# Roots of norms by Newton steps on token partitions in the attention stage of a Hymba layer

## The chip, the cores and the metric

The kernel runs on one core of one Trainium2 chip. The metric is the device time of one execution in microseconds (us). The engines are TensorE (PE; its weight loads are listed as PEld), VectorE (DVE), ScalarE (ACT), GpSimd (POOL) and SyncE (SP, which here starts DMA transfers). Each engine works through its own queue in order and waits on semaphores for the others.

## The reference

One layer with two feed-forward blocks around two groups of attention heads, all in float32, on 1024 tokens and 16 meta tokens. What matters here are the norms behind the two groups:

```python
def rmsnorm(x, g):
    xf = x.astype(jnp.float32)
    y = xf * lax.rsqrt(jnp.mean(xf * xf, axis=-1, keepdims=True) + EPS)
    return (y * g.astype(jnp.float32)).astype(x.dtype)
...
    p = jax.nn.softmax(s, axis=-1)
    a = p[:, :, 0] - lam * p[:, :, 1]            # differential attention, 4 heads
...
    o = rmsnorm(o, sub_gain) * (1.0 - lambda_init)   # per head, over its 128 features
...
    out_b = rmsnorm(out_b, win_norm[l])              # window group, over 512 features
    h = h + jnp.concatenate([out_a, out_b], axis=-1) @ w_out[l]
```

## The kernel before

All large products are made of three products of rounded parts: each factor is split into a high part (a cast) and a low part (a subtraction), and hi·hi, lo·hi and hi·lo are added in PSUM. Activations lie transposed: features on the 128 partitions, tokens along the free axis. The program is written with a framework whose scheduler orders each engine's queue; tiles of one name share a ring of buffers.

The change lies in the differential stage, which the profiled execution passes at 1060 to 1331 us. Its loop takes one step `i` for each of 32 query tiles (4 heads × 8 tiles) and four more. A step issues:

- the scores of a tile, `ds` (L780, PE), the row minimum `dmx` (L784, DVE), the exponential `dp` with its sum (L786, ACT), and one step later the difference of the two softmaxes (L791 and L794 on DVE, L793 on POOL);
- the transposes `dt` of the difference of an earlier tile (L1167, L1175, PE) and their copies to `at` (L1170 on DVE, L1172 and L1176 on ACT);
- in every second step the products with the values, `do<-at,v` (L1183), copied to the head's `oh` (L1186, ACT); in the other steps, from step 9, a piece of `out_win`, the products of the window group with its output weights (`do<-ow_hi,owhi` and so on, L167), whose results DVE adds to `hrm` (L114);
- at i = 4 and 8 the norm of one half of the window group (`own`, four tiles of 128 features), and from i = 7, every fourth step, the norm of half a head (`oh`, 512 tokens).

`do` and `dt` have one PSUM buffer each; `do` is shared by the values, the window-out products and the sums of the norms.

A norm before: ACT squares the tile (`nacc`; for the window group POOL adds four of them), PE multiplies the result with a matrix of ones (L1092, 128x512), so that every partition has the sum of its token. ACT takes the root (`nr`, L1097, Abs_reciprocal_sqrt), for which its table is loaded, and the exponential's table is loaded again afterwards. ACT squares the root (`nt`, L1101), and two DVE operations correct it by a Newton step (L1102, L1103). POOL multiplies the tile by the root (L1112, L1122), ACT makes the high part with the gain (L1114, L1124), DVE the low part (L1115, L1125). For heads 0 to 2 ACT copies the sums of both halves to `nv` (L1139), and one root of 1024 columns serves the pair; head 3 has a root for each half. Behind the loop the remaining `fill` steps follow, and then the output products of the differential group (`po`, L167); `s`, `wal` and `wah` are the parts of the next block's weights, which SP loads (`s<-wu`).

Of the kernel before, what the change touches and what calls it, by code (L numbers as in the profile page):

```python
# [10 lines left out]
F32 = mybir.dt.float32  # L11
F32R = mybir.dt.float32r
AF = mybir.ActivationFunctionType
ALU = mybir.AluOpType
# [4 lines left out]
P = 128  # L19
# [32 lines left out]
def layer(  # L52
# [40 lines left out]
    gains = const("gains", [P, 4, KT])  # L93
    eps = cpool.tile([P, 1], F32, name="eps")
    nc.vector.memset(eps, EPS)
    warm = cpool.tile([P, 1], F32, name="warm")
    nc.scalar.activation(warm, eps, AF.Abs_reciprocal_sqrt)
    nc.vector.tensor_scalar(gains, gains, -0.5 / D, None, op0=ALU.mult)

    wgain = const("wgain", [P, 4])  # L100
    dgain = const("dgain", [P, 1])
    nc.vector.tensor_scalar(wgain, wgain, -0.5 / 512, None, op0=ALU.mult)
    nc.vector.tensor_scalar(dgain, dgain, -0.5 / P * (1.0 - LAMBDA_INIT), None, op0=ALU.mult)

    neglam = cpool.tile([P, 1], F32, name="neglam")

# [6 lines left out]
    def tt(eng, out, a, b, op):  # L113
        eng.tensor_tensor(out, a, b, op=op)  # L114

    def split(hi, lo, src, eng=None):
        nc.scalar.copy(hi, src)  # L117
        tt(eng or nc.vector, lo, src, hi.bitcast(F32), ALU.subtract)
# [953 lines left out]
    owp = Rings(st_o, "ow").reserve("owraw").reserve("owhi", 2).reserve("owlo", 2)  # L1072
    with ExitStack() as st:
        op = Rings(st, "op").reserve("ow_hi").reserve("ow_lo")
        npool = Rings(st, "dn")
        psum = Rings(st, "dps", space=PSUM).reserve("do").reserve("dt")
        ds1 = Rings(st, "ds1", space=PSUM).reserve("ds")

        ow_hi = op.tile([P, 4, SEQ], F32R, name="ow_hi")
        ow_lo = op.tile([P, 4, SEQ], F32R, name="ow_lo")  # L1080

        def sums(srcs, n):
            acc = npool.tile([P, 512], F32, tag="nacc", name="nacc")[:, :n]
            for i, s in enumerate(srcs):
                if i == 0:
                    nc.scalar.activation(acc, s, AF.Square)
                else:
                    sq = npool.tile([P, 512], F32, tag="nsq", name="nsq")[:, :n]
                    nc.scalar.activation(sq, s, AF.Square)
                    nc.gpsimd.tensor_tensor(acc, acc, sq, op=ALU.add)  # L1090
            ps = psum.tile([P, 512], F32, tag="do", name="do")[:, :n]
            nc.tensor.matmul(ps, ones, acc, start=True, stop=True)  # L1092
            return ps

        def rsqrt(v, n, width):
            r = npool.tile([P, SEQ], F32, tag="nr", name="nr")[:, :n]
            nc.scalar.activation(r, v, AF.Abs_reciprocal_sqrt, bias=eps, scale=1.0 / width)  # L1097
            for c0 in range(0, n, 512):
                vc, rc = v[:, c0 : c0 + 512], r[:, c0 : c0 + 512]
                t = npool.tile([P, 512], F32, tag="nt", name="nt")  # L1100
                nc.scalar.activation(t, rc, AF.Square)  # L1101
                nc.vector.scalar_tensor_tensor(t, vc, EPS * width, t, op0=ALU.add, op1=ALU.mult)  # L1102
                nc.vector.scalar_tensor_tensor(rc, t, -3.0 * width, rc, op0=ALU.add, op1=ALU.mult)  # L1103
            return r

        def win_norm(c):
            c0, n = CH_REAL[c]
            ow = npool.tile([P, 4, 512], F32, tag="own", name="own")
            nc.sync.dma_start(ow, ow_d[:, :, c0 : c0 + n])
            r = rsqrt(sums([ow[:, t, :] for t in range(4)], n), n, 512)  # L1110
            for t in range(4):
                nc.gpsimd.tensor_tensor(ow[:, t, :], ow[:, t, :], r, op=ALU.mult)  # L1112
                hi = ow_hi[:, t, c0 : c0 + n]
                nc.scalar.mul(hi, ow[:, t, :], wgain[:, t : t + 1])  # L1114
                nc.vector.scalar_tensor_tensor(  # L1115
                    ow_lo[:, t, c0 : c0 + n], ow[:, t, :], wgain[:, t : t + 1], hi.bitcast(F32),
                    op0=ALU.mult, op1=ALU.subtract,
                )

        def head_scale(hd, c, o, r):  # L1120
            c0, n = CH_REAL[c]
            nc.gpsimd.tensor_tensor(o, o, r, op=ALU.mult)  # L1122
            hi = o_hi[:, hd, c0 : c0 + n]
            nc.scalar.mul(hi, o, dgain)  # L1124
            nc.vector.scalar_tensor_tensor(  # L1125
                o_lo[:, hd, c0 : c0 + n], o, dgain, hi.bitcast(F32), op0=ALU.mult, op1=ALU.subtract
            )

        nvs = {}

        def head_norm(hd, c, oh):
            os = [oh[:, c0 : c0 + n] for c0, n in CH_REAL]
            ps = sums([os[c]], 512)
            if hd == 3:
                head_scale(hd, c, os[c], rsqrt(ps, 512, P))
                return
            if c == 0:
                nvs[hd] = npool.tile([P, SEQ], F32, tag="nv", name="nv")
            nc.scalar.copy(nvs[hd][:, c * 512 : (c + 1) * 512], ps)  # L1139
            if c == 1:  # L1140
                r = rsqrt(nvs[hd], SEQ, P)
                for j in range(2):
                    head_scale(hd, j, os[j], r[:, j * 512 : (j + 1) * 512])

        def out_win(m, c, ws):
            if c == 0:
# [51 lines left out]
        for i in range(NQ + 4):  # L1198
            work, tg = None, iter(())
            steps = []  # L1200

            def do_scores(c):
                if N_EARLY <= i < NQ:
                    scores(heads[i // NB], i % NB, c, sc[i], ds1 if c else ds0)

            def do_combine():
                if N_EARLY < i <= NQ:
                    pend[i - 1] = combine(*sc.pop(i - 1))

# [24 lines left out]
            do_scores(0)  # L1234
            do_scores(1)
            do_combine()
            for z in range(3):
                do_t()
                if z < 2:
                    do_w()  # L1240
            if i < NQ and i % NB == 4 and i // NB + 1 < 4:
                heads[i // NB + 1] = load_head(i // NB + 1)
            if i in (4, 8):
                win_norm(i // 8)
            if i >= 7 and (i - 7) % 4 == 0:
                hd2, c = divmod((i - 7) // 4, 2)
                head_norm(hd2, c, ohs[hd2])
        for _ in fill:
            pass

# [165 lines left out]
```

## Time and profile before

| | |
|---|---|
| time, median of 3 runs | 2071.48 us (2070.87 to 2072.05) |
| profiled execution | 2074.79 us, its span 2072.9 us |
| mean granted TensorE clock | 0.981 of full speed |
| PE busy in the span | 1943.9 us (94%) |
| DVE, ACT, POOL busy | 1279.3 (62%), 879.4 (42%), 960.3 (46%) us |
| of it in 1066 to 1331 us: PE | 232.25 of 265 us |
| DVE, ACT, POOL there | 178.60, 163.44, 104.24 us |

Busy times are those of instructions on the engine; a matmul's end is modelled. The span runs from the first to the last instruction, the time of an execution also has what lies around it. The last two lines are the stage of the change.

### The profile page before, as it was taken

How to read it: one execution, taken by the hardware profiler on the slowest of the kernel's cores; microseconds unless marked ns; L12 is line 12 of the kernel's file. 1: busy time of each engine (PE TensorE's matmuls, PEld its weight loads, DVE VectorE, ACT ScalarE, POOL GpSimd, SP SyncE). 2: the span in 40 equal slices, each digit the busy share in tenths (PEclk: the TensorE clock that was granted, in tenths of full speed). 3: DMA queues.
4: the chain of work that ended last, by engine and by line, in shares of the span. 5: the costliest groups of instructions: out<-in, count | busy, mean ns of one | idle time of the engine just before them, and what ended most of it. 6: DMA issues, size and time to landing. Idle time of an engine off the chain costs nothing.

```text
span 2072.9 us, 30356 instructions
## 1 busy us (share of the span) xinstructions
PE 1943.9 (94%) x11484; PEld 1692.1 (82%) x11484; DVE 1279.3 (62%) x1853; ACT 879.4 (42%) x1611; POOL 960.3 (46%) x807
## 2 busy tenths in 40 slices
PE   5999999998999989899978999898999999989998
PEld 4999999998999879777756777676778888877877
DVE  7855554548875660376766777477665555487745
ACT  6433333334432431366566666354333333344433
POOL 0565454545443740576456432003655554454443
PEclk9999999999999999999988999999999999999999
DMA  5332322328422351544442321622323223375122
GB/s 172 108 109 98 120 92 97 109 92 319 155 64 81 133 174 52 143 122 123 105 113 67 97 85 39 203 102 81 124 106 122 95 89 117 130 282 167 61 82 82
DMA packets 106003, 244.14 MB, mean 118 GB/s; under 512 B 14209, under 2 KB 29009, under 8 KB 105857
## 3 DMA queue, kind: packets, MB, share of 16 engines
q1 hardware_dynamic: 94336, 204.53, 31.1%
q0 software_dynamic: 11520, 37.67, 4.6%
q8 instruction: 90, 1.47, 0.3%
q14 instruction: 57, 0.46, 0.1%
HBM read 169.86 MB, written 65.44 MB: 114 GB/s over the span
## 4 chain that ended last, share of the span: by engine, by line
PE 70%; DVE 11%; DMA 6%; ACT 5%; POOL 3%; issue 3%; SPq 1%; DVEq 0%; POOLq 0%; ACTq 0%
PE p L226 35%; PE pA L577 7%; PE pj L167 5%; PE pC L577 3%; PE pv L884 3%; PE pd L167 2%; PE ds L780 2%; DVE bl L114 2%; PE po L167 2%; PE do L1183 2%; PE pB L577 2%; PE do L167 1%; DMA ru<-wu 1%; POOL s L114 1%; ACT dp L786 1%
## 5 line engine op out<-in xcount | busy, mean ns | idle before, releaser
L114 POOL TENSOR_TENSOR s<-ru 128x512 f32<-128x512 f32 x42 | 55.9, 1331 | 264.5 <-DMA ru<-wu 190.1
L226 PE MATMUL p<-b_hi,wal 128*128 128x260 f32 (+1 forms) x528 | 141.5, 323 | 5.7 <-DVE wal L114 5.7
L226 PE MATMUL p<-b_hi,wah 128*128 128x260 f32 (+1 forms) x528 | 143.2, 325 | 3.6 <-ACT wah L117 1.6
L226 PE MATMUL p<-t_hi,wch 128*128 128x260 f32 (+1 forms) x528 | 141.2, 321 | 5.7 <-DVE u L114 5.7
L226 PE MATMUL p<-b_lo,wah 128*128 128x260 f32 (+1 forms) x528 | 142.5, 322 | 3.4 <-DVE b_lo L114 3.4
L226 PE MATMUL p<-t_lo,wch 128*128 128x260 f32 (+1 forms) x528 | 141.0, 321 | 0.0
L226 PE MATMUL p<-t_hi,wcl 128*128 128x260 f32 (+1 forms) x528 | 140.8, 321 | 0.0
L226 PE MATMUL p<-t_lo,wbh 128*128 128x260 f32 (+1 forms) x504 | 135.5, 319 | 0.0
L226 PE MATMUL p<-t_hi,wbl 128*128 128x260 f32 (+1 forms) x504 | 133.4, 320 | 0.0
L226 PE MATMUL p<-t_hi,wbh 128*128 128x260 f32 (+1 forms) x504 | 133.1, 320 | 0.0
L114 DVE TENSOR_TENSOR u<-p,m 128x520 f32<-128x520 f32 (+1 forms) x88 | 61.0, 693 | 116.5 <-PE p L226 108.9
L117 ACT CAST wbh<-s 128x512 fp32r<-128x512 f32 x84 | 52.1, 621 | 164.9 <-PE p L226 142.1
L577 PE MATMUL pA<-bh,wh 128*128 128x260 f32 (+1 forms) x432 | 115.3, 322 | 2.6 <-DVE h L584 2.6
L577 PE MATMUL pA<-bl,wh 128*128 128x260 f32 (+1 forms) x432 | 114.7, 319 | 0.0
L117 ACT CAST wah<-rg 128x512 fp32r<-128x512 f32 x88 | 53.9, 620 | 143.0 <-PE p L226 112.1
L577 PE MATMUL pA<-bh,wl 128*128 128x260 f32 (+1 forms) x432 | 111.9, 319 | 1.8 <-POOL wl L114 1.8
L114 DVE TENSOR_TENSOR wal<-rg,wah 128x512 fp32r<-128x512 f32 x88 | 74.0, 847 | 63.6 <-ACT wah L117 63.6
L114 DVE TENSOR_TENSOR bl<-r,bh 128x520 fp32r<-128x520 f32 (+1 forms) x126 | 109.0, 900 | 3.3 <-ACT bh L117 2.6
L117 ACT CAST wch<-ru 128x512 fp32r<-128x512 f32 x88 | 54.7, 621 | 130.5 <-PE p L226 72.6
L584 DVE SCALAR_TENSOR_TENSOR h<-pA,h 128x520 f32<-128x520 f32 (+1 forms) x96 | 66.1, 690 | 63.2 <-PE pA L577 63.1
L117 ACT CAST wh<-s 128x384 fp32r<-128x384 f32 x96 | 49.1, 513 | 130.1 <-PE pA L577 65.5
L114 POOL TENSOR_TENSOR s<-wr 128x384 f32<-128x384 f32 x48 | 55.4, 1157 | 100.6 <-DVE wl L114 89.7
(290 smaller groups left out, 6113.2 us busy)
## 6 DMA issues: line engine op xcount, KB each, us to landing
rg<-wg SPq DMA_DIRECT2D x44, 512.0 KB, 3.6
ru<-wu SPq DMA_DIRECT2D x44, 512.0 KB, 5.0
wr<-wd SPq DMA_DIRECT2D x24, 768.0 KB, 4.4
r<-g_t SPq DMA_DIRECT2D x12, 780.0 KB, 5.8
r<-g_t SPq DMA_DIRECT2D x12, 768.0 KB, 5.3
g_b<-g POOLq DMA_DIRECT2D x27, 260.0 KB, 5.2
r<-g_b SPq DMA_DIRECT2D x9, 780.0 KB, 6.4
g_b<-g POOLq DMA_DIRECT2D x27, 256.0 KB, 5.1
```

The source lines that it names most:

```text
L114: eng.tensor_tensor(out, a, b, op=op)
L117: nc.scalar.copy(hi, src)
L167: nc.tensor.matmul(o, w, x[:, c0 : c0 + n], start=first and i == 0, stop=last and i == 2)
L226: nc.tensor.matmul(o, w_k(ww, k), x[:, k, c0 : c0 + cn], start=first and k == 0 and i == 0, stop=k == hk - 1 and i == 2, skip_group_check= ...
L577: nc.tensor.matmul(o, w_k(ww, k), xx[:, c0 : c0 + cn], start=new and k == 0 and q == 0, stop=k == DNG - 1 and q == 2, skip_group_check=not ...
L584: nc.vector.scalar_tensor_tensor(hs, full, 0.5, hs, op0=ALU.mult, op1=ALU.add)
L780: nc.tensor.matmul(o, qs[c][:, qt * P : (qt + 1) * P], kk[:, c0 : c0 + n], start=i == 0, stop=i == 1)
L786: nc.scalar.activation(p, full, AF.Exp, bias=mx, scale=-1.0, accum_out=z[:, c : c + 1])
L884: nc.tensor.matmul(ps[:m, 192 + c * 320 : 512 + c * 320], u[:, k, sl], w[:, k, c * 320 : (c + 1) * 320], start=k == 0 and i == 0, stop=k = ...
L1183: nc.tensor.matmul(po[:, :256], v[:m, j, :], at[:m, j, :], start=j == 0, stop=j == NB)
```

## The change

The sums of a norm are taken with the tokens on partitions: for each block of 128 tokens the squares `acc` are the weights and one column of ones is passed, so that a [128, 4] tile holds the sums of 512 tokens. On it DVE makes the reciprocal root: a first guess by integer arithmetic on the bits (`ny`), then three Newton steps of three small operations. POOL multiplies the identity by each of the four columns, which gives four diagonal blocks `ndg`. In a later step of the loop PE multiplies ones with `ndg`, which brings the roots to all partitions with the tokens along the free axis again. DVE scales the tile with root and gain in one operation that reads PSUM; ACT casts the high part, and POOL subtracts for the low part. Each norm is a generator in the list `norms`, and `do_norms` moves each one stage forward in each step. The window norms are started at i = 3 and 7 instead of 4 and 8, `nacc` has two buffers, the pair roots of heads 0 to 2 are gone. The gains are scaled for the plain root.

```diff
+    eps4 = cpool.tile([P, 4], F32, name="eps4")
+    nc.vector.memset(eps4, EPS)
...
-        def sums(srcs, n):
...
-            ps = psum.tile([P, 512], F32, tag="do", name="do")[:, :n]
-            nc.tensor.matmul(ps, ones, acc, start=True, stop=True)
+        def rsqrt(acc, width, e):
+
+            ps = psum.tile([P, 512], F32, tag="do", name="do")
+            for j in range(4):
+                nc.tensor.matmul(ps[:, j : j + 1], acc[:, j * P : (j + 1) * P], ones[:, 0:1], start=True, stop=True)
+            v, y, t = (npool.tile([P, 4], F32, tag=n, name=n) for n in ("nv", "ny", "nt"))
+            nc.vector.scalar_tensor_tensor(v, ps[:, 0:4], 1.0 / width, e, op0=ALU.mult, op1=ALU.add)
+            nc.vector.tensor_scalar(
+                y.bitcast(I32), v.bitcast(I32), -0.5, float(0x5F3759DF), op0=ALU.mult, op1=ALU.add
+            )
+            for _ in range(3):
+                tt(nc.vector, t, y, y, ALU.mult)
+                nc.vector.scalar_tensor_tensor(t, t, -0.5, v, op0=ALU.mult, op1=ALU.mult)
+                nc.vector.scalar_tensor_tensor(y, t, 1.5, y, op0=ALU.add, op1=ALU.mult)
+            dg = npool.tile([P, 512], F32, tag="ndg", name="ndg")
+            for j in range(4):
+                nc.gpsimd.tensor_scalar(
+                    dg[:, j * P : (j + 1) * P], ident, y[:, j : j + 1], 1.0, op0=ALU.mult, op1=ALU.mult
+                )
+            yield
+            ps = psum.tile([P, 512], F32, tag="do", name="do")
+            nc.tensor.matmul(ps, ones, dg, start=True, stop=True)
             return ps
 
-        def rsqrt(v, n, width):
-            r = npool.tile([P, SEQ], F32, tag="nr", name="nr")[:, :n]
-            nc.scalar.activation(r, v, AF.Abs_reciprocal_sqrt, bias=eps, scale=1.0 / width)
-            for c0 in range(0, n, 512):
-                vc, rc = v[:, c0 : c0 + 512], r[:, c0 : c0 + 512]
-                t = npool.tile([P, 512], F32, tag="nt", name="nt")
-                nc.scalar.activation(t, rc, AF.Square)
-                nc.vector.scalar_tensor_tensor(t, vc, EPS * width, t, op0=ALU.add, op1=ALU.mult)
-                nc.vector.scalar_tensor_tensor(rc, t, -3.0 * width, rc, op0=ALU.add, op1=ALU.mult)
-            return r
+        def scaled(o, g, r, hi, lo):
+            nc.vector.scalar_tensor_tensor(o, r, g, o, op0=ALU.mult, op1=ALU.mult)
+            split(hi, lo, o, nc.gpsimd)
...
+        def head_norm(hd, c, oh):
...
+            nc.scalar.activation(acc, o, AF.Square)
+            yield
+            r = yield from rsqrt(acc, P, eps4)
+            scaled(o, dgain, r, o_hi[:, hd, c0 : c0 + n], o_lo[:, hd, c0 : c0 + n])
+
+        norms = []
+
+        def do_norms():
+            for g in list(norms):
+                if next(g, norms) is norms:
+                    norms.remove(g)
...
-            if i in (4, 8):
-                win_norm(i // 8)
+            do_norms()
+            if i in (3, 7):
+                norms.append(win_norm(i // 7))
+                next(norms[-1])
             if i >= 7 and (i - 7) % 4 == 0:
                 hd2, c = divmod((i - 7) // 4, 2)
-                head_norm(hd2, c, ohs[hd2])
+                norms.append(head_norm(hd2, c, ohs[hd2]))
+                next(norms[-1])
+        while norms:
+            next(fill, None)
+            next(fill, None)
+            do_norms()
```

The order of ACT at the norm of head 1 (its second half) stood as follows before; `dp` are exponentials, `at` copies of transposes, `nv`, `nr` and `nt` the norm.

```order
L1139 COPY nv<-do 128x512
L1172 COPY at<-dt 128x4x128
L786 ACTIVATE dp_14144,dz<-ds,dmx_14142 128x1040
L1097 ACT_TABLE_LOAD
L1097 ACTIVATE nr<-nv,eps 128x1024
L1101 ACTIVATE nt<-nr 128x512
L1176 COPY at<-dt 16x128
L786 ACT_TABLE_LOAD
L786 ACTIVATE dp_14051,dz<-ds,dmx_14049 128x1040
L1101 ACTIVATE nt<-nr 128x512
L786 ACTIVATE dp_14210,dz<-ds,dmx_14208 128x1040
L1186 COPY oh<-do 128x256
```

Now ACT has there (`owhi` is a cast of window-out weights, `nacc` the squares of the next half, lines are one higher):

```order
L787 ACTIVATE dp_14084,dz<-ds,dmx_14082 128x1040
L1177 COPY at<-dt 16x128
L787 ACTIVATE dp_14020,dz<-ds,dmx_14018 128x1040
L118 CAST o_hi<-oh 128x512
L787 ACTIVATE dp_14146,dz<-ds,dmx_14144 128x1040
L1187 COPY oh<-do 128x256
L1134 ACTIVATE nacc<-oh 128x512
L118 CAST owhi<-owraw 128x512
L1173 COPY at<-dt 128x4x128
L1177 COPY at<-dt 16x128
```

The copies of the sums, both table loads, the root and its squares are gone; a cast stands between two exponentials.

On PE the sum at a half of head 1 was one product between transposes, scores and values:

```order
L1167 MATMUL dt<-ident,dp_13612 128x128 x4
L1092 MATMUL do<-nacc,ones 128x512
L780 MATMUL ds<-kh,qst 128x264
L780 MATMUL ds<-kh,qst 128x512
L780 MATMUL ds<-kh,qst 128x264
L780 MATMUL ds<-kl,qst 128x264
```

Now four one-column products stand in its place, and behind the 12 window-out products and six of scores that follow them the product with the diagonal stands between transposes:

```order
L1168 MATMUL dt<-ident,dp_14020 128x128 x4
L1089 MATMUL do<-ones,nacc 128x1 x4
L1176 MATMUL dt<-ident,dp_14020 16x128
L1168 MATMUL dt<-ident,dp_14073 128x128 x4
L168 MATMUL do<-ow_hi,owhi 128x512
```

```order
L781 MATMUL ds<-kl,qst 128x264
L1168 MATMUL dt<-ident,dp_14073 128x128 x4
L1106 MATMUL do<-ndg,ones 128x512
L1176 MATMUL dt<-ident,dp_14073 16x128
L1168 MATMUL dt<-ident,dp_14135 128x128 x4
L1184 MATMUL do<-at,v 128x256 x9
```

What moved: the norm takes `do` twice, with DVE's and POOL's part of the root between the two.

On DVE at the end of the stage (`hrm` the window-out sums, `s` the difference for the next block's weights, `wal` a low part of them) stood:

```order
L1102 SCALAR_TENSOR_TENSOR nt<-do,nt 128x512
L114 TENSOR_TENSOR ha<-po,ha 128x512
L1103 SCALAR_TENSOR_TENSOR nr<-nt,nr 128x512
L114 TENSOR_TENSOR hrm<-do,hrm 128x512
L1125 SCALAR_TENSOR_TENSOR o_lo<-oh,dgain,o_hi 128x512
L114 TENSOR_TENSOR s<-s 128x512 x2
L114 TENSOR_TENSOR wal<-rg_15659,wah 128x512
L114 TENSOR_TENSOR hrm<-do,hrm 128x512
```

and now:

```order
L1098 SCALAR_TENSOR_TENSOR ny<-nt,ny 128x4
L115 TENSOR_TENSOR hrm<-do,hrm 128x512
L115 TENSOR_TENSOR owlo<-owraw,owhi 128x512
L1110 SCALAR_TENSOR_TENSOR oh<-do,dgain,oh 128x512
L115 TENSOR_TENSOR owlo<-owraw,owhi 128x512
L115 TENSOR_TENSOR wal<-rg_15845,wah 128x512
L115 TENSOR_TENSOR owlo<-owraw,owhi 128x512
L115 TENSOR_TENSOR s<-s 128x512
```

The last `hrm` now stands ahead of `s` and of the last head's scaling.

## Rows read from the trace of the kernel before

**Rows 1.** Stretches of the stage: start:end, length, busy per engine, PEclk, DMA share, GB/s.
```profile
1066.00:1150.40 84.40, 68.79 (x311) 53.77 (x312) 57.47 (x66) 56.58 (x98) 43.86 (x29) 0.84 0.20 57
1150.40:1268.00 117.60, 110.29 (x590) 88.49 (x589) 86.12 (x101) 76.30 (x137) 46.50 (x30) 1.00 0.26 77
1268.00:1331.00 63.00, 53.16 (x254) 39.65 (x252) 35.00 (x46) 30.55 (x54) 13.87 (x10) 1.00 0.37 118
```
**Rows 2.** PE's waits, 1150.4 to 1268: total us, times, longest.
```profile
PE ds L780 <- ACT dp L786: 4.5, 7, 0.9
PE dt L1167 <- ACT at L1176: 2.5, 4, 1.1
```
**Rows 3.** Timeline of PE behind the second head pair: start, us, idle before.
```profile
1217.61 0.74 PE L780 MATMUL ds<-kh,qst 128*128 128x264 f32 x3 [0.67 <-ACT dp L786]
...
1224.40 0.66 PE L1167 MATMUL dt<-ident,dp 128*128 128x128 f32 x4 [1.12 <-ACT at L1176]
1225.52 0.75 PE L780 MATMUL ds<-kh,qst 128*128 128x264 f32 x3 [0.45 <-ACT dp L786]
```
**Rows 4.** Groups of ACT by form, 1066 to 1331: busy us, mean ns, idle before.
```profile
L1097 ACT ACT_TABLE_LOAD x6 | 7.7, 1283 | 0.1
L786 ACT ACT_TABLE_LOAD x5 | 6.4, 1283 | 0.1
L1101 ACT ACTIVATE nt<-nr 128x512 f32<-128x512 f32 x10 | 6.3, 627 | 0.2
...
L1139 ACT COPY nv<-do 128x512 f32<-128x512 f32 x6 | 3.5, 584 | 2.7 <-PE do L1092 2.6
L1097 ACT ACTIVATE nr<-nv,eps 128x1024 f32<-128x1024 f32 x3 | 3.5, 1151 | 0.0
```
**Rows 5.** Timelines of PE and of ACT at the window norms.
```profile
1088.11 0.75 PE L780 MATMUL ds<-kh,qst 128*128 128x264 f32 x3 [2.89 <-ACT dp L786]
...
1117.29 1.11 PE L1167 MATMUL dt<-ident,dp 128*128 128x128 f32 x4 [3.08 <-ACT at L1176]
...
1116.03 1.04 ACT L759 CAST qst<-qraw 128x1024 fp32r<-128x1024 f32 x1 [1.71 <-DMA qraw<-qa_d]
```
**Rows 6.** Groups of DVE by form, 1066 to 1331.
```profile
L784 DVE TENSOR_REDUCE dmx<-ds 128x1 f32<-128x1040 f32 x60 | 73.9, 1236 | 21.3 <-PE ds L780 20.9
...
L1102 DVE SCALAR_TENSOR_TENSOR nt<-do,nt 128x512 f32<-128x512 f32 x4 | 2.8, 690 | 3.5 <-ACT nt L1101 3.5
```
**Rows 7.** Tile rz (ns min/median/max), and timelines of DVE and POOL at its longest.
```profile
L987 DVE TENSOR_TENSOR rz<-z,es x16: 146/164/2116, 880.9 to 1037.5; 128x4 f32<-128x4 f32 x16
...
1037.48 2.09 DVE L987 TENSOR_TENSOR rz<-z,es 128x4 f32<-128x4 f32 x1
...
1037.14 2.42 POOL L114 TENSOR_TENSOR kl<-kraw,kh 128x1040 fp32r<-128x1040 f32 x1
```
**Rows 8.** Groups of POOL by form, whole execution.
```profile
L793 POOL TENSOR_SCALAR dp<-dp,drz,neglam 128x1040 f32<-128x1040 f32 x32 | 40.9, 1277 | 75.3 <-DVE drz L791 74.8
...
L990 POOL TENSOR_SCALAR p<-p,rz 128x272 f32<-128x272 f32 x16 | 7.6, 489 | 2.5 <-DVE rz L988 2.5
```
**Rows 9.** The chain, 1190 to 1212: start, us, what, so many instructions.
```profile
1204.40 0.44 PE dt L1167 x4
1204.84 2.77 PE do L167 x12
1207.60 0.11 PE dt L1175
1207.71 0.95 PE ds L780 x6
1208.67 0.87 PE do L1092 x2
```
**Rows 10.** The chain at the stage's end, and PE's timeline behind it.
```profile
1324.61 3.64 DMA s<-wu
...
1331.06 0.47 PE L167 MATMUL po<-o_hi,owhi 128*128 128x512 f32 x1 [2.50 <-DVE hrm L114]
```
**Rows 11.** A stretch of the second feed-forward's start, columns as in rows 1.
```profile
1345.00:1360.00 15.00, 15.00 (x66) 12.06 (x65) 7.30 (x11) 3.64 (x6) 0.00 (x0) 1.00 0.28 106
```

More of the change, by code (lines that the diff above doesn't have):

```diff
@@ L101, in layer @@
     dgain = const("dgain", [P, 1])
-    nc.vector.tensor_scalar(wgain, wgain, -0.5 / 512, None, op0=ALU.mult)
-    nc.vector.tensor_scalar(dgain, dgain, -0.5 / P * (1.0 - LAMBDA_INIT), None, op0=ALU.mult)
+    nc.vector.tensor_scalar(dgain, dgain, 1.0 - LAMBDA_INIT, None, op0=ALU.mult)
     neglam = cpool.tile([P, 1], F32, name="neglam")
@@ L1074, in layer @@
         op = Rings(st, "op").reserve("ow_hi").reserve("ow_lo")
-        npool = Rings(st, "dn")
+        npool = Rings(st, "dn").reserve("nacc", 2)
         psum = Rings(st, "dps", space=PSUM).reserve("do").reserve("dt")
@@ L1080, in layer @@
         ow_lo = op.tile([P, 4, SEQ], F32R, name="ow_lo")
-        def sums(srcs, n):
[L1083 to L1090, printed above, removed]
-            ps = psum.tile([P, 512], F32, tag="do", name="do")[:, :n]
-            nc.tensor.matmul(ps, ones, acc, start=True, stop=True)
-            return ps
@@ L1095, in rsqrt @@
-        def rsqrt(v, n, width):
-            r = npool.tile([P, SEQ], F32, tag="nr", name="nr")[:, :n]
-            nc.scalar.activation(r, v, AF.Abs_reciprocal_sqrt, bias=eps, scale=1.0 / width)
-            for c0 in range(0, n, 512):
-                vc, rc = v[:, c0 : c0 + 512], r[:, c0 : c0 + 512]
-                t = npool.tile([P, 512], F32, tag="nt", name="nt")
-                nc.scalar.activation(t, rc, AF.Square)
-                nc.vector.scalar_tensor_tensor(t, vc, EPS * width, t, op0=ALU.add, op1=ALU.mult)
-                nc.vector.scalar_tensor_tensor(rc, t, -3.0 * width, rc, op0=ALU.add, op1=ALU.mult)
-            return r
+        I32 = mybir.dt.int32
@@ L1109, in win_norm @@
             nc.sync.dma_start(ow, ow_d[:, :, c0 : c0 + n])
-            r = rsqrt(sums([ow[:, t, :] for t in range(4)], n), n, 512)
+            acc = npool.tile([P, 512], F32, tag="nacc", name="nacc")
             for t in range(4):
[L1112 to L1118, printed above, removed]
@@ L1120, in head_scale @@
-        def head_scale(hd, c, o, r):
-            c0, n = CH_REAL[c]
[L1122 to L1143, printed above, removed]
+                if t == 0:
+                    nc.scalar.activation(acc, ow[:, t, :], AF.Square)
+                else:
+                    sq = npool.tile([P, 512], F32, tag="nsq", name="nsq")
+                    nc.scalar.activation(sq, ow[:, t, :], AF.Square)
+                    nc.gpsimd.tensor_tensor(acc, acc, sq, op=ALU.add)
@@ new lines, in win_norm @@
+            yield
+            r = yield from rsqrt(acc, 512, eps4)
+            for t in range(4):
+                scaled(ow[:, t, :], wgain[:, t : t + 1], r, ow_hi[:, t, c0 : c0 + n], ow_lo[:, t, c0 : c0 + n])
+        def head_norm(hd, c, oh):
+            c0, n = CH_REAL[c]
+            o = oh[:, c0 : c0 + n]
+            acc = npool.tile([P, 512], F32, tag="nacc", name="nacc")
+            nc.scalar.activation(acc, o, AF.Square)
+            yield
+            r = yield from rsqrt(acc, P, eps4)
+            scaled(o, dgain, r, o_hi[:, hd, c0 : c0 + n], o_lo[:, hd, c0 : c0 + n])
```

## The prediction

> **What bounds the kernel now.** I read the page's busy shares first (PE works 94% of the span), then the table by stretches for the differential stage alone, then PE's waits there, then the timeline around a norm. The stage has three characters [rows 1]. In 1066–1150.4 PE works 68.79 of 84.40 us at a mean granted clock of 0.84. In 1150.4–1268 it works 110.29 of 117.60 at clock 1.00: here PE itself is the limit, and only the 7.3 us in which it stands can be won by any change of other engines. In 1268–1331 it works 53.16 of 63.00. ACT, with 163 us of 265, is the next engine. In the middle stretch nearly all of PE's waits are for ACT: 4.5 us for exponentials dp and 2.5 us for a copied tile at [rows 2].
>
> The timeline says where those waits sit. At the second head pair PE stands 0.67, then 1.12, then 0.45 us, all behind ACT [rows 3], directly after the root of that pair. The first pair has four such waits of 2.12 together, the third has three of 2.20. ACT's own account gives the reason [rows 4]: six table loads for the root (7.7 us), five to get the exponential's table back (6.4), ten squares (6.3), six copies of sums (3.5), the three long roots (3.5). ACT's queue is in order, so the exponentials that PE needs for its next transposes stand behind a load, a root of 1.15 us, a square and the second load.
>
> **The change, part by part.** Signs are microseconds of the profiled execution (2074.79; its span is 2072.9). It lies 3.3 above the median of the runs, 2071.48, so I take 3.3 off at the end.
>
> *(a) Head pairs 0 to 2 lose loads, root, squares and nv copies on ACT.* In the order of ACT all of it is gone between the dp rows, and a cast of the head stands there instead of a multiplication with the gain: one for one. The three groups of waits are 2.12, 2.24 and 2.20: −6.5. Below, nothing, if PE then waits at the same places for something else; above, −9, if the other 2 us of waits for ACT in the middle stretch go as well [rows 2].
>
> *(b) The window norms lose the same*, in the clock-poor first stretch. The first one's root made PE stand 2.89 us for a dp at 1088.11 [rows 5]. The other large wait there, 3.08 at 1117.29, is behind a copy on ACT that stood behind the cast of qst, and that cast waited 1.71 us for its DMA [rows 5]; the change doesn't touch it. I take −2.9. From −6 (both go) to +8: the new norm needs the one "do" buffer twice instead of once, with a chain of DVE, POOL, PE and DVE, and if every value product of tiles 4 to 10 slips by a stage of that chain, a few waits of 2 us come in.
>
> *(c) New products.* The sum over features was one 128x512 product (two passes, 0.87 us [rows 9]); now the product with the diagonal has that shape and costs the same 0.87. The four one-column products are extra. Each loads its block as weights and passes one column. No row shows that shape; the nearest are the transposes, where four weight loads with 128 columns take 0.44, 0.11 each [rows 9]. A full-precision product is two passes, so 8 × 0.11 = 0.87 a norm. Seven of the ten norms lie where PE is the limit: +6.1. Lower bound 0 (hidden in other waits), upper 8.4, by the mean weight load of the middle stretch, 88.49/589 = 0.15, times 8 and 7 [rows 1].
>
> *(d) The tail.* DVE's last hrm addition stands behind s, which waits 3.64 us for the load of wu, so that PE stands 2.50 before the next po products [rows 10]. In the new order of DVE s comes behind all hrm rows. −2.5; bounds 0, if the last head's longer norm chain takes its place, and −4.
>
> *(e) New waits at the norms.* Between the one-column products and the product with the diagonal PE has, by the order, one small transpose, four more, 12 window-out products, 6 score products and 4 transposes: 0.11 + 0.44 + 2.77 + 0.95 + 0.44 = 4.7 us [rows 9]. The chain to be hidden under it: 11 DVE operations on 128x4. The row nearest is rz, 128x4, median 0.164 [rows 7]: 1.8 us. Then four POOL operations of 128x128: POOL's one-operand forms take 1.277 for 1040 columns and 0.489 for 272 [rows 8], about 1.03 ns a column, so 128 columns take 0.34 (at most 0.49): 1.4 us, at most 2.0. Together 3.2, with hand-overs some 3.5. Slack 1.2 us, about one DVE operation of 1.24 [rows 6] in front. Behind the diagonal's product "do" is busy until DVE has scaled from it (0.69, as the operation nt that reads do [rows 6]), while PE has five transposes, 0.55 [rows 9], before the value products that need "do": 0.2 each, seven times, +1.4. Lower bound 0, upper 9 (DVE in the middle of a 1.24 us reduction each time, 7 × 1.3).
>
> One rule speaks against this part. Rows first: one 128x4 multiplication of two SBUF tiles at 1037.48 took 2.09 us where the median is 0.164, while POOL's kl subtraction ran from 1037.14 for 2.42 [rows 7]. The Trainium skill ("SBUF — State Buffer", section "SBUF: two separate sides") has the rule: a DVE operation with two SBUF inputs and a GpSimd operation that reads SBUF share one port pair as an exclusive lock, held for the whole instruction. By it a Newton chain can be stopped once for a whole POOL operation; the trace agrees in that one row. By the median row the chain is 1.8 us, by the rule up to 2 more where POOL is busy; that is the slower rival below.
>
> Edits at no cost: DVE's totals. Per norm it loses two operations and the subtraction for lo, all of 512 columns and of 0.69 or more [rows 6], so at least 2.1 us, and gains the 11 small ones and one of 0.69, 2.5 us; it works 179 of 265 us, and what it lags behind is priced in (e). POOL gains the diagonals and lo, and works 104 of 265 us in the stage [rows 1]. One table load moves into the second feed-forward's first root: PE works 15.00 of 15.00 us at 1345–1360 [rows 11], so it is covered; uncovered it would be 1.28 [rows 4].
>
> *Sum:* −6.5 − 2.9 + 6.1 − 2.5 + 1.4 = −4.4, so 2070.4 for the profiled execution and **2067** as the median.
>
> **Rivals.**
>
> *No change.* PE is the limit and the products give back what the waits gave: (c) and (e) near their middle-to-upper values, 8.4 and 3.5, against −6.5 − 2.9 − 2.5: 0. **2071.5.** For it: the middle stretch works 94% of the time. Against: 0.15 for a load hidden under another pass is an upper figure.
>
> *Slower.* The norm chain is longer than its cover. Place: the diagonal's product, which stands in order on PE with dt and value products behind it. Price: each norm of the ten overshoots by one POOL or DVE operation of 1.24 to 1.28 [rows 6, 8], +13 in all: 2067 + 13 = **2080**. It decides once the chain is over 4.7 us, i.e. from 1.2 us above my 3.5. For it: the stopped rz row, and POOL at 40% busy. Against: POOL's operations in the middle stretch are few (30 in 118 us [rows 1]).
>
> *Larger gain.* ACT loses some 30 us in the stage. If dp is then always in time, the 15.6 us that PE stands in the first stretch and the clock of 0.84 there come back in part: half of the 15.6 more than counted, **2058**. For it: PE's first-stretch waits are mostly for ACT. Against: the same stretch is also paced by loads [rows 5].
>
> **How the numbers follow.** Forecast 0.45, within 2062 to 2071 by the bounds of (c) and (e); no change 0.20; slower 0.17; larger gain 0.18. 0.2% of this kernel is 4.1 us, about what a measurement can tell from no change: 2067.3 to 2075.6. The forecast lies at its lower edge; about seven tenths of its weight are below it. Faster 0.45 × 0.7 + 0.18, near 0.50; same 0.45 × 0.3 + most of 0.20, 0.29; slower the rest, 0.21. The range takes in both outer cases to their centre: 2057 to 2080.
>
> **What the new profile would show.** (a) No table load in the stage, and no wait over 0.5 us for dp in the step behind a head pair. (b) The wait of 2.89 at the first window norm gone. (c) Four one-column products in 0.9 us, PE's busy time in the middle up by about 0.9 a norm. (d) No wait of PE for hrm behind the load of wu. (e) The diagonal's product waiting under 0.5 us for POOL. I am wrong if PE waits over 1 us at each diagonal's product or for "do" behind it, if the small DVE operations take well over 0.164, or if the POOL diagonals take over 0.5 each.

## The result, and the profile after

The change makes the kernel slower: 2105.03 us median of four runs (2098.53 to 2108.24) against 2071.77 (2070.87 to 2076.78); the ratio is 1.0148, with a 95% interval from 1.0131 to 1.0166. The forecast was 2067 with a range of 2057 to 2080, so the time lies 25 us above the range. The profiled execution took 2108.24 us, 33.5 more than the one before (2074.79).

The stretches of the stage after the change, to be read beside [rows 1] (same columns: length, busy time of PE, PEld, DVE, ACT, POOL, then the granted clock). The stretches lie later and don't hold the same work: the middle one has 195 passes of score products before and 132 after, the last one 35 and 72. So they are to be read by their shares and clocks:

```profile
1063.18:1155.00 91.82, 71.83 (x349) 56.75 (x350) 65.38 (x104) 51.07 (x95) 45.64 (x41) 0.85 0.23 67
1155.00:1268.00 113.00, 101.04 (x514) 79.11 (x512) 71.82 (x106) 51.34 (x97) 48.97 (x40) 0.97 0.29 85
1268.00:1358.78 90.78, 80.85 (x380) 62.30 (x380) 50.65 (x96) 30.69 (x64) 20.38 (x28) 0.94 0.29 93
```

ACT has lost its load, as forecast. But PE, which ran at 94% and clock 1.00 in the middle before, now stands more (89%) and runs part of the middle and the end at a lower clock. The waits of PE after the window norms, 1155 to 1345 (total us, times, longest):

```profile
PE dt L1168 <- ACT at L1177: 3.8, 10, 0.5
PE dt L1176 <- DVE at L1171: 3.8, 4, 1.3
PE ds L781 <- ACT dp L787: 2.9, 7, 0.5
PE do L1106 <- POOL ndg L1101: 1.9, 2, 1.4
PE do L1184 <- DVE oh L1110: 1.5, 3, 0.7
```

[Rows 2] has the middle stretch alone. Before the change the part behind the window norms, 1144 to 1317.8, had:

```profile
PE ds L780 <- ACT dp L786: 5.7, 9, 0.9
PE dt L1167 <- ACT at L1176: 5.5, 8, 1.1
PE dt L1175 <- DVE at L1170: 0.8, 1, 0.8
```

After the change no wait for `dp` from 1155 us on is longer than 0.5 us: the waits behind the pair roots [rows 3] are gone. In their place stand waits for DVE's copies `at`, for the diagonal, and for `do` behind DVE's scaling.

Over the whole stage, from the first score product to the unbroken run of `po` products, the sums are these. PE waits 16.3 us for `dp` before and 15.2 after, 11.9 and 10.7 for ACT's copies `at`, 3.4 and 7.1 for DVE's copies `at`, 1.5 and 9.3 ahead of products into `do`, 3.0 and 2.0 ahead of `po`. In the first stretch the 2.89 us at the first window norm became 0.74, but other waits came in (2.19 for `dp` at 1130.33, 2.01 for ACT's copy `oh` at 1113.97), so that the waits for `dp` in the first part (up to 1150.4 and 1155) are 10.6 us before and 12.2 after. The groups of PE in the stage, with the new products and their waits:

```profile
L1106 PE MATMUL do<-ndg,ones 128*128 128x512 f32 x20 | 11.3, 648 | 3.2 <-POOL ndg L1101 1.9 <-DVE hrm L115 1.3
...
L1089 PE MATMUL do<-ones,nacc 128*128 128x1 f32 x80 | 10.3, 250 | 0.3 <-ACT oh L1187 0.3
L1176 PE MATMUL dt<-ident,dp 128*16 128x128 f32 x32 | 8.9, 279 | 8.9 <-DVE at L1171 5.9 <-ACT at L1173 3.0
```

And DVE's small operations, to be read beside [rows 7], with the combination of the two softmaxes (43.7 us in all, 1365 ns the mean, before):

```profile
L795 DVE SCALAR_TENSOR_TENSOR dp<-dp,drz,dp 128x1040 f32<-128x1040 f32 x32 | 48.9, 1529 | 13.4 <-POOL dp L794 13.2
...
L115 DVE TENSOR_TENSOR nt<-ny 128x4 f32<-128x4 f32 x30 | 8.2, 273 | 0.9
...
L1098 DVE SCALAR_TENSOR_TENSOR ny<-nt,ny 128x4 f32<-128x4 f32 x30 | 5.8, 194 | 0.8
L1097 DVE SCALAR_TENSOR_TENSOR nt<-nt,nv 128x4 f32<-128x4 f32 x30 | 5.6, 187 | 0.7
```

**Where the time went.** I take the stage in each profiled execution from the first score product to the last wait ahead of the unbroken run of `po` products, and in slices of 5 us multiply PE's busy time by the granted clock. That gives three parts: PE standing, PE's work as it would be at full clock, and what the lower clock added. A stage is that of one profiled execution, which lay up to 7 us from the median beside it (E6 6.7 above, E15 6.9 below, the others within 4).

| kernel (median us of the runs) | stage | PE stands | work at full clock | lost to the clock |
|---|---|---|---|---|
| before (2071.8) | 286.5 | 38.6 | 236.2 | 11.7 |
| after (2105.0) | 313.5 | 46.6 | 249.2 | 17.7 |
| E1 without columns (2088.4) | 298.8 | 49.0 | 234.8 | 15.0 |
| E2 columns doubled (2119.6) | 324.3 | 43.8 | 255.5 | 25.0 |
| E3 diagonal a step later (2091.7) | 296.0 | 41.0 | 246.7 | 8.3 |
| E4 no root (2076.8) | 285.3 | 41.7 | 234.4 | 9.2 |
| E5 before, no table loads (2067.3) | 279.7 | 33.5 | 235.4 | 10.8 |
| E6 no columns, no Newton steps (2076.4) | 283.6 | 40.0 | 234.4 | 9.2 |
| E10 a step later, no columns (2109.8) | 315.7 | 58.4 | 239.0 | 18.2 |
| E15 no root, in one piece (2065.4) | 271.8 | 31.0 | 235.1 | 5.7 |
| E16 sums a step earlier (2103.7) | 313.4 | 47.7 | 245.8 | 19.9 |
| E17 all in one piece (2132.3) | 344.4 | 64.0 | 251.1 | 29.2 |

So of the 27 us that the stage grew, 13 are PE's own work, 8 are waits and 6 are clock. Another 5.7 us lie behind the stage, 3 of them clock and 3 work, less a shorter wait. These can't be laid to the change with certainty: ahead of the stage, where both kernels run the same 7166 passes, the same division gives 976.7 and 971.4 us of work and 9.7 and 16.5 lost to the clock. So work holds to about half a percent, 1 to 2 us in the stage, and what the clock takes differs between executions by itself.

The clock can be seen to fall behind a norm's columns at 1265, in PE's timeline:

```profile
1265.63 0.95 PE L1089 MATMUL do<-ones,nacc 128*128 128x1 f32 x8
1266.44 0.27 PE L1176 MATMUL dt<-ident,dp 128*16 128x128 f32 x1
1267.06 0.66 PE L1168 MATMUL dt<-ident,dp 128*128 128x128 f32 x4 [0.34 <-ACT at L1177]
1268.17 1.04 PE L781 MATMUL ds<-kh,qst 128*128 128x264 f32 x3 [0.46 <-ACT dp L787]
1269.01 1.07 PE L781 MATMUL ds<-kl,qst 128*128 128x264 f32 x3
```

Eight short passes, a few transposes, two waits, and the next score products take 1.04 and 1.07 where 0.74 and 0.64 are usual: the granted clock, 1.00 up to 1268.0, is 0.50 from 1268.5 to 1271.5 and 1.00 again from 1272.0, that is, from 2.4 to 1.2 GHz and back. From 1150 us to the stage's end the kernel before has no such fall, nor have E1, E4 and E6, which have no columns; the changed kernel has five of some 4 us each (8.3 us lost), E2 seven (11.9), E3 two (3.3). The columns are not the only way to it: two of the five falls come within 3 us of a norm's columns, and E10, which has no columns but long waits, has five falls as well (7.4 us).

### The profile page after: what moved, and what is told of

Its sections match the earlier page's. It is cut to its first block, busy times and chain, and to the rows that moved or that the text cites. A ratio compares the mean times of both kernels' runs of the same rounds, so it can differ in the third digit from the quotient of the medians.

```text
span 2106.4 us, 30625 instructions
## 1 busy us (share of the span) xinstructions
PE 1971.0 (94%) x11564; PEld 1710.5 (81%) x11564; DVE 1284.6 (61%) x1943; ACT 850.6 (40%) x1578; POOL 967.9 (46%) x847
## 4 chain that ended last, share of the span: by engine, by line
PE 70%; DVE 10%; issue 7%; DMA 5%; ACT 4%; POOL 3%; SPq 1%; DVEq 0%; POOLq 0%; ACTq 0%
PE p L227 37%; PE pA L578 7%; PE pj L168 4%; PE pC L578 3%; PE do L1184 3%; PE pv L885 3%; PE pd L168 2%; PE ds L781 2%; DVE bl L115 2%; PE pB L578 2%; PE do L168 1%; ACT dp L787 1%; DVE dmx L785 1%; PE wo L1018 1%; DMA wdraw<-wd 1%
## 5 line engine op out<-in xcount | busy, mean ns | idle before, releaser
L227 PEld LDWEIGHTS p<-t_hi,wch 128*128 128x128 f32 x528 | 88.0, 190 | 16.8 <-DVE u L115 8.7
```

Of the source, the lines that this page charges most:

```text
L227: nc.tensor.matmul(o, w_k(ww, k), x[:, k, c0 : c0 + cn], start=first and k == 0 and i == 0, stop=k == hk - 1 and i == 2, skip_group_check= ...
```

## The experiments

Two theories stood against each other at first: that the **columns** cost TensorE time and clock, and that the buffer **do**, taken twice a norm, holds up the value products, so that both halves of a pair's values lie in one piece (10 of 16 pairs by the order, against 2 before) and no longer cover the copies of the transposes.

**E1, the one-column products left out.**

```diff
-            ps = psum.tile([P, 512], F32, tag="do", name="do")
-            for j in range(4):
-                nc.tensor.matmul(ps[:, j : j + 1], acc[:, j * P : (j + 1) * P], ones[:, 0:1], ...)
-            nc.vector.scalar_tensor_tensor(v, ps[:, 0:4], 1.0 / width, e, ...)
+            nc.vector.scalar_tensor_tensor(v, acc[:, 0:4], 1.0 / width, e, ...)
```

> The four one-column products of each norm are left out, so the sums are not taken (the root is made of four columns of the squares); every other operation stays, and the buffer do is taken once a norm instead of twice. By the order, the two halves of the value products then stand together in 2 of 16 pairs, against 10 in the changed kernel and 2 in the kernel before. Theory 1, the products themselves cost TensorE time and clock: 10 x 0.95 = 9.5 us directly and some of the clock, so 2090 to 2096. Theory 2, the buffer do held twice a norm delays the value products so that they lie in one piece and no longer cover the copies of the transposes: nearly all comes back, 2066 to 2076.

2088.37 us (ratio to before 1.0071, 1.0046 to 1.0096): 17 less, and 17 still there. PE's work is 234.8, that of before; its waits stay. That is just below theory 1's range. Columns, with the first taking of `do` that goes with them, are about half the loss; with 2 pairs in one piece instead of 10, theory 2 in its strong form falls.

**E2, the columns doubled** (the `matmul` line twice).

> The four one-column products are issued twice (the second time into the same columns, so the result is the same). Theory 1, the products themselves are the cost: 9 to 10 us more, and some us of clock, 2114 to 2122. Theory 2, the buffer is the cost: do is held only 0.9 us longer, with 9 of 16 pairs in one piece as against 10, so at most the direct 9 us and no more clock, 2105 to 2114.

2119.59 us (1.0216, 1.0188 to 1.0245): 14.6 more, in theory 1's range. In the stage 6 us are added as work and 7 as clock, and PE stands 3 less; theory 1 had 9 to 10 us of work and some of clock. The profiled execution is only 11.6 us longer than that of the changed kernel.

```profile
1042.80:1367.11 324.31, 280.50 (x1386) 220.61 (x1384) 198.49 (x318) 147.32 (x275) 128.69 (x116) 0.91 0.28 83
```

This row of the view by stretches is the whole stage of E2: 280.5 us busy, at a mean clock of 0.91.

**E3, the product with the diagonal a step later** (a second `yield` ahead of it).

> The product with the diagonal is issued one loop step later (one more yield); the same instructions, in another order: the halves of the value products stand together in 4 of 16 pairs, against 10. Theory 1, the products are the cost: unchanged, 2100 to 2107. Theory 2, the buffer do taken again too early is the cost: 10 to 25 us less, 2080 to 2095.

2091.74 us (1.0079, 1.0051 to 1.0106): 13.3 less, with the same instructions. The columns' work remains (246.7); waits and clock are nearly those of before. That is in theory 2's range: two fifths of the loss go with the order of the same instructions.

**E4, no root at all.** The one product that is left takes the squares; columns, small operations and diagonals are left out, and the sums stand for the roots.

```diff
-            nc.tensor.matmul(ps, ones, dg, start=True, stop=True)
+            nc.tensor.matmul(ps, ones, acc, start=True, stop=True)
```

> No root at all: ones times the squares goes into do where the product with the diagonal stood, and DVE scales with the sums; left out are the one-column products, the eleven small DVE operations, the POOL diagonals. It bounds what this arrangement of the loop can give: no table load, no columns, no chain. Both theories: the waits behind the old roots are gone, so below the kernel before; theory 1 2060 to 2066, theory 2 the same. If it is not below 2070, the table loads were no cost, and the first term of the forecast was wrong by itself.

2076.82 us (1.0022, 1.0004 to 1.0039): not below the kernel before. By what was expected here, the table loads would then have been no cost; E5 and E15 speak against that. Its trace shows what stands where the roots were, at the second head's norm; PE first, then DVE, then POOL in their timelines:

```profile
1228.12 0.28 PE L1159 MATMUL dt<-ident,dp 128*16 128x128 f32 x1 [1.61 <-DVE at L1154]
...
1224.38 1.24 DVE L785 TENSOR_REDUCE dmx<-ds 128x1 f32<-128x1040 f32 x1 [0.20 <-PE ds L781]
1225.53 1.93 DVE L795 SCALAR_TENSOR_TENSOR dp<-dp,drz,dp 128x1040 f32<-128x1040 f32 x1
1227.38 0.68 DVE L1154 COPY at<-dt 128x512 f32<-128x512 f32 x1
...
1225.10 1.26 POOL L115 TENSOR_TENSOR o_lo<-oh,o_hi 128x512 fp32r<-128x512 f32 x1 [0.66 <-ACT o_hi L118]
```

PE waits 1.61 us for the copy `at`, which stands behind DVE's row minimum and combination. The combination took 1.93, while POOL's new subtraction for `o_lo` ran into it. Three heads show the same wait of 1.6. The longest wait stands at the end of the stage: 5.26 us at 1332.69, behind the cast `owhi` of weights that come late.

**E5, the kernel before without its table loads.** The same instructions in the same order on every engine; the norms' values are others.

```diff
-            nc.scalar.activation(r, v, AF.Abs_reciprocal_sqrt, bias=eps, scale=1.0 / width)
+            nc.scalar.activation(r, v, AF.Exp, bias=eps, scale=-1.0 / width)
```

> The kernel before with the exponential in place of the reciprocal root in its norms (other values, so the outputs are not the reference's; same instructions in the same order on every engine). Only the eleven table loads of the stage are gone, 14 us of ACT. Theory A (terms a and b of the forecast): the loads with the root held up the exponentials; without them 4 to 7 us less, 2065 to 2069. Theory B: behind ACT stands the next limit, DVE and TensorE themselves, so nothing measurable comes back: within 2 us of the kernel before.

2067.33 us (0.9972, 0.9957 to 0.9987): 6.0 less than the 2073.37 of before on that chip, in theory A's range. PE's waits from 1144 to the first `po` product at 1308.9:

```profile
PE dt L1167 <- ACT at L1176: 4.8, 8, 1.1
PE ds L780 <- ACT dp L786: 2.8, 5, 0.8
```

The waits for `dp` are half of the 5.7 us that the same part has before; those for `at` hardly move. Together E4 and E5 say that the new arrangement, doing less than E5, takes 9.5 us more.

**E6, E1 without Newton steps, and E7, E1 with the diagonals on ACT.**

```diff
-            for _ in range(3):
+            for _ in range(0):          # E6
...
-                nc.gpsimd.tensor_scalar(dg[...], ident, y[:, j : j + 1], 1.0, ...)
+                nc.scalar.mul(dg[...], ident, y[:, j : j + 1])          # E7
```

> The run without one-column products, and without the three Newton steps as well (nine small DVE operations a norm less; the first guess is used as it is). Left are the two first DVE operations and the POOL diagonals. If the chain on DVE made the 12 us between the run without columns (2088.4) and the run without any root (2076.8), this gives 2076 to 2080. If the POOL diagonals or the order made it, 2084 to 2089.

> The run without one-column products, with the four diagonal blocks made by ACT instead of POOL; everything else as there. If POOL is at fault (its operations and DVE's with two SBUF inputs stop each other, and the diagonals wait in POOL's queue in front of the softmax combination), a good part of the 12 us comes back: 2077 to 2083. If only the DVE chain counts, 2086 to 2090.

E6: 2076.42 us (1.0016, 1.0001 to 1.0031). Without the 90 small operations the 12 us are gone; the guess and the POOL diagonals, which E6 keeps, cost nothing beside E4. In E1 the small operations ran far longer than by the median of 0.16:

```profile
L1094 DVE SCALAR_TENSOR_TENSOR nt<-nt,nv 128x4 f32<-128x4 f32 x30 | 11.0, 366 | 0.7
L115 DVE TENSOR_TENSOR nt<-ny 128x4 f32<-128x4 f32 x30 | 9.9, 332 | 0.9
L1095 DVE SCALAR_TENSOR_TENSOR ny<-nt,ny 128x4 f32<-128x4 f32 x30 | 9.0, 301 | 0.8
```

That is 29.9 us of DVE. PE's waits show where taking them away helped: 4.3 us less for `dp`, whose row minima stand in DVE's queue, 3.0 less behind `hrm`, 1.5 less for DVE's copies `at`. E7: 2091.54 us (1.0085, 1.0068 to 1.0102): POOL's making of the diagonals was not at fault. But E7 is no test of whether POOL slows DVE's small operations: they still take 28.9 us there, and each of the slow ones stands beside another POOL operation (`kl`, `qst`, `owlo`, one `dp`).

**E8, E4 with the low parts on DVE** (`split(hi, lo, o)` instead of `split(hi, lo, o, nc.gpsimd)`).

> The run without any root (sums used in place of the root, one product of ones and squares), with the low parts of the norms subtracted by DVE, as in the kernel before, instead of POOL. There DVE's combination of the two softmaxes took 1.93 us where POOL's subtraction for o_lo ran, and TensorE stood 1.6 us behind it at each head. If that port conflict ate the gain, 3 to 6 us less than 2076.8: 2070 to 2074. If not, 2075 to 2078, or above, because DVE has more to do.

2079.82 us (1.0025, 1.0012 to 1.0039). The conflict that E4's rows show is real: without it the waits of 1.6 us at these heads are 0.98. But the kernel gained nothing; in E8 the wait at the end is 6.5 us instead of 5.3.

**E9, E1 with the Newton steps on POOL** (`tt(nc.gpsimd, ...)` and one `tensor_scalar`, four operations a step).

> The run without one-column products, with the three Newton steps on POOL (four small POOL operations a step instead of three of DVE). The chain is longer in time, but DVE has nine operations a norm less. If the 12 us of the steps are DVE's occupied time (the copies of the transposes and the row minima stand behind them), they come back: 2075 to 2081. If they are the length of the chain in front of the product with the diagonal, or if small POOL operations stop DVE's, nothing comes back or it gets worse: 2087 to 2096.

2083.37 us (1.005, 1.0032 to 1.0067): 5 of the 12 us come back by the medians, between the two theories; the intervals of E1 and E9 overlap, those of E6 and E9 don't. So taking the steps off DVE did not give all of it back. PE now waits 3.4 us in all for the diagonals, which it didn't in E1; that is the longer chain, but POOL has more to do as well, and the run doesn't separate the two.

**E10, E3 without the columns** (both edits).

> The run with the product with the diagonal one step later, and without the one-column products. In the run with them TensorE was busy 232.8 us at full clock in the stage against 222.8 before, and waits and clock were no worse than before. If the columns cost there only their time on TensorE, 9 to 11 us less than 2091.7: 2080 to 2083. If they cost it twice, as in the changed kernel (17 us), 2073 to 2077. If the order alone was the cost of holding do, 2086 to 2089, as the run without columns.

2109.84 us (1.0171, 1.0145 to 1.0197), against all expectations: with less to do, 18 us more than E3. Timelines of PE, of DVE and of POOL at the norm there:

```profile
1158.21 0.28 PE L1174 MATMUL dt<-ident,dp 128*16 128x128 f32 x1 [3.67 <-DVE at L1169]
...
1165.78 2.08 PE L1104 MATMUL do<-ndg,ones 128*128 128x512 f32 x2 [3.48 <-POOL ndg L1098]
...
1154.21 0.99 DVE L1094 SCALAR_TENSOR_TENSOR nt<-nt,nv 128x4 f32<-128x4 f32 x1
...
1155.20 2.36 DVE L785 TENSOR_REDUCE dmx<-ds 128x1 f32<-128x1040 f32 x2
1157.49 0.67 DVE L1169 COPY at<-dt 128x512 f32<-128x512 f32 x1
...
1153.91 2.50 POOL L115 TENSOR_TENSOR ow_lo<-own,ow_hi 128x512 fp32r<-128x512 f32 x2 [5.62 <-ACT ow_hi L118]
```

The scheduler put row minima and small operations ahead of the copy for which PE stands 3.67 us, and small operations of the next norm between; one of 0.16 takes 0.99 while POOL subtracts. Waits are 58.4 us. An edit here is worth what the new order makes of it.

**E11, only the head norms changed** (window norms as before, at steps 4 and 8, with their table loads).

> Only the eight head norms are changed, the two window norms are those of the kernel before (their sums, roots, table loads and their place at steps 4 and 8). If the cost goes by the number of norms, 8/10 of 33 us stay: 2096 to 2101. If the window norms with do taken twice were the large part (term b's upper bound, 8 us), 2085 to 2094. If they were a gain (term b as forecast), 2105 to 2110.

2099.44 us (1.0116, 1.0093 to 1.0139): as for a loss that goes by the number of norms. The window norms were neither a gain nor the main loss.

**E12, the product with the diagonal in dt** (`tag="dt"` instead of `tag="do"`).

> The changed kernel with one word altered: the product with the diagonal goes into the buffer dt of the transposes instead of do, so that a norm takes do once (for the sums) and dt once. All instructions are the same; by the order the halves of the value products stand together in 1 of 16 pairs, against 10. If do taken twice, and the value products in one piece, were a cost of their own beside the columns and the chain, 2088 to 2096, as in the run with the product one step later (2091.7). If that run gained by its later place alone, 2100 to 2107. If dt is worse to hold than do (transposes queue behind DVE's scaling), above 2107.

2095.66 us (1.0108, 1.009 to 1.0125): 9.4 less, as for a cost of `do` taken twice. But E16 below bounds that reading.

**E13 to E15, what costs the new arrangement 9.5 us where no root is taken.** E13 is E5 with a root for each half of every head (`if hd >= 0`), E14 is E4 with `if i in (4, 8)`, E15 is E4 without its two `yield`s.

> The kernel before with the exponential in place of the root (no table loads) and with a root for each half of every head, as head 3 has it, instead of one for the pair; still in one piece where the squares are taken. If a norm for each half is what costs the new arrangement its 9.5 us (2076.8 without any root against 2067.3 without table loads), this gives 2074 to 2080. If the halves are no cost, 2064 to 2070.

> The run without any root, with the window norms started at steps 4 and 8 as in the kernel before, instead of 3 and 7. If the earlier window norms cost the 9.5 us, 2067 to 2072; if not, 2075 to 2079.

> The run without any root, with each norm issued in one piece at the step of its squares, as in the kernel before, instead of over three steps. If the spreading over the steps costs the 9.5 us, 2066 to 2072; if not, 2075 to 2079.

E13: 2084.1 us (1.0067, 1.0045 to 1.0089), above both ranges. E14: 2074.98 (1.0011, 0.9996 to 1.0025). E15: 2065.42 (0.9965, 0.9953 to 0.9978), 11.4 less than E4 by the order alone: PE stands 31.0 us instead of 41.7. It was the order that goes with spreading a norm over three steps: the waits for DVE's copies `at` are 4.1 us instead of 9.1, and the wait at the end for `owhi` 0.8 instead of 5.3. E13's 17 us above E5 come with three more roots on ACT; it shows that halves are dear with such a root, not that they cost E4 anything.

**E16 to E18, the same remedy on the changed kernel.** E16 issues the sums in the step of the squares (without the first `yield`), E17 the whole norm (without both), E18 is E16 with the Newton steps on POOL.

> The changed kernel with the sums issued in the step of the squares instead of the next one; the product with the diagonal stays a step later. All instructions are the same; by the order the halves of the value products stand together in 3 of 16 pairs, against 10. If the spreading over the steps costs what the runs without a root show (11 us), and do taken twice some 10, 2085 to 2095. If the place of the sums doesn't matter, 2100 to 2107.

> The changed kernel with each whole norm issued in one piece at the step of its squares, the remedy that took 11 us from the run without a root. All instructions are the same, but here do is taken twice with the small operations and the diagonals between; by the order the value products stand in one piece in 15 of 16 pairs. If spreading is bad in itself, 2090 to 2097. If it is bad for a norm that takes do once and needed for one that takes it twice, 2110 to 2130.

> The best valid form that the runs point to: sums in the step of the squares, and the Newton steps on POOL instead of DVE (5 us less in the run without columns). If both hold together, 2080 to 2090, still above the kernel before, since the one-column products alone keep TensorE 10 us longer. If the longer chain of small POOL operations isn't covered here, above the run with the sums moved alone.

E16: 2103.68 us (1.0151, 1.0133 to 1.017), no gain. E17: 2132.3 (1.0284, 1.0265 to 1.0303): the remedy turns round where `do` is taken twice with a chain between, PE stands 64.0 us, 15.2 of them ahead of the small transpose for DVE's copies. E18: 2100.08 (1.0126, 1.0108 to 1.0145), above the 2080 to 2090 of both gains together. E16 has 3 of 16 pairs in one piece, E3 4, and E16 is 12 us slower: the pieces are not what decides. No version here that computes the norms beats the kernel before.

## Why the prediction was wrong

**In the terms of the sum.** (a), (b), (d) and (e) together were to take 10.5 us from PE's waits; the waits grew by 8.0. (c) was to add 6.1 us of work; it added 13.0. The clock stood at nothing; it took 6.0 more.

**The step that failed is the account of DVE** ("Edits at no cost: DVE's totals") together with (e). I compared sums, 2.1 us lost against 2.5 gained per norm, and called DVE covered. The sum was about right: DVE is busy 192.2 us in the stage before and 199.4 after. But what DVE gained is a chain in its queue, with row minima, `hrm` and copies `at` behind it, for which the exponentials and PE wait. E6 against E1 sizes the steps: 12 us, where nothing stood. By the medians their own time is 90 × 0.163 = 14.7 us; in the changed kernel they took 19.6, in E1 29.9. E9 leaves open how much of the 12 is DVE's time, how much the chain's length and how much the order.

(a) and (b): the mechanism was right, the size two thirds of it. Without the loads alone the kernel gains 6.0 us (E5) where −9.4 stood; without any root, in one piece, 6 to 7 (E15). In the changed kernel little of that gain is left: the waits for `dp` and for ACT's copies fell by 2.3 us together, and the norm spread over three steps costs 11.4 (E15 against E4). (a) also counted waits of 0.35 and 0.46 us as those of the root; the changed kernel, which has no root on ACT, still has such waits, as at 1267 and 1268 above.

(c) was mis-sized by a factor of two: 6.1 forecast, 13.0 of work measured, and 10.5 in E3. The price of one norm was right where the products run undisturbed, 0.80 us for eight passes on the chain:

```profile
1351.19 0.80 PE do L1089 x8
```

But the work grew by 1.05 to 1.3 us for each of ten norms, and the forecast took seven. The clock was left out: 6 us in the stage, 7 more when the columns are doubled.

(d) came about as put: the last `hrm` no longer waits. What is late next had not been named: the cast of the weights `owhi`, behind the load of `owraw` (1.56 us here, 5.26 in E4). So the waits ahead of `po` fell by 1.0 us, not 2.5.

(e) The waits at `do` came to 9.3 us against 1.5 before, 7.8 more, near the upper bound of 9 instead of the 1.4 that I took. My cover of 4.7 us for the chain was fair: PE waited only 1.9 us for the diagonals.

By the medians, none of the signs of being wrong came up: two of the ten diagonal products waited for POOL, 1.4 us the longer, the small operations have medians of 0.161 to 0.163, the POOL diagonals one of 0.372. And what the new profile was to show came nearly as put. The signs looked at the norms' own products and operations; the loss stood in passes and clock summed over the stage, and in waits elsewhere.

The slower rival (2080) had the right sign, but a quarter of the size, and its place was wrong: not the product with the diagonal decides, but the columns with the clock, and the waits at `do` and behind DVE. The rule of the Trainium skill ("SBUF — State Buffer", section "SBUF: two separate sides") that a DVE operation of two SBUF inputs and a GpSimd operation that reads SBUF lock each other out is borne out by the trace: six Newton operations of the changed kernel take 0.98 to 1.01 us where the medians are 0.161 to 0.163, and each ends with the POOL multiplication `dp` (L794) beside it. That makes 4.9 us of DVE's time in all. It is not the bulk of the changed kernel's loss: in E2, which is slower still, it makes 2.1 us. How much of E1's 12 us it makes is not shown: there the same stretching is 15.2 us, E7 left it in place, and E8 has no Newton operations.

Put together, the levels are: 2067 without the loads (E5), 2077 spread over steps without a root (E4), 2076 with guess and diagonals (E6), 2088 with the Newton steps (E1), 2105 with the columns. They are levels of orders as much as prices: E10 has less in it than E3 and takes 18 us more. What stays open is how much of the 12 and of the 17 us belongs to the work, how much to POOL's operations beside DVE's, and how much to the order that the scheduler made.

## What to carry to other kernels

Where PE is busy 94% of a stretch, count every pass that a change adds for every time it runs, and read what a lower clock would add; a wait removed is worth at most what the next engine leaves of it. Small operations on an engine whose results TensorE waits for are to be priced by what stands behind them in the queue, not by their sum. And where a scheduler orders the queues, test an edit in two orders before giving it a price: one `yield` moved this kernel by 13 us one way, and by 21 us the other way once the columns were gone (E10 against E1).

## What was not expected of the hardware

The granted clock fell in the middle of a well-filled stage, in the place shown behind short products and waits of half a microsecond each: the mean clock of the stage went from 0.95 to 0.93, and to 0.91 when the one-column products were doubled, where the stage had 7 us more lost to the clock. A 128x4 operation on DVE, 0.16 us by the median, took up to 1.0 us beside POOL in the changed kernel and 2.4 in E1.
